# A hybrid gMLP and state-space block: the strips of squares of y are multiplied directly behind the products inside a chunk

## The chip, the cores and the metric

The kernel is one program on one core of a Trainium2 chip. The metric is the time of that core in microseconds, read on the device. Before the change it is 1373.79 us, the median of three runs between 1373.0 and 1373.83 us. TensorE is called PE in the profile (its weight loads have a row of their own, PEld), VectorE DVE, ScalarE ACT, GpSimd POOL, and SyncE, which issues most loads, SP.

## The reference

One layer on 1024 positions of width 1024. An input product feeds a chunked gMLP branch (`y_a`) and a Mamba-2 state-space branch (`y_b`); both are projected, gated, added and projected again.

```python
proj = h @ w_in
gm_u, gm_v, gm_z, ssm_z, xbc, dt_raw, g_a, g_b = jnp.split(proj, SPLITS, axis=-1)
y_a = spatial_gating(jax.nn.gelu(gm_u), jax.nn.gelu(gm_v), gm_ln_w, gm_ln_b, gm_ws, gm_bs) * jax.nn.silu(gm_z)
xbc = jax.nn.silu(causal_depthwise_conv(xbc, conv_w, conv_b))
...
y_b = ssd_scan(xh, dt, a, bm.reshape(b, s, SSM_GROUPS, SSM_STATE), cm.reshape(b, s, SSM_GROUPS, SSM_STATE))
y_b = y_b + xh * d_skip[:, None]
yz = (y_b.reshape(b, s, SSM_D_INNER) * jax.nn.silu(ssm_z)).reshape(b, s, SSM_GROUPS, SSM_D_INNER // SSM_GROUPS)
y_b = rms_norm(yz, ssm_norm_w.reshape(SSM_GROUPS, -1)).reshape(b, s, SSM_D_INNER)
merged = jax.nn.sigmoid(g_a) * (y_a @ w_proj_a) + jax.nn.sigmoid(g_b) * (y_b @ w_proj_b)
return x + gate[:, None, :] * (merged @ w_out)
```

and inside `ssd_scan`, with chunks of 128 positions, 8 groups (g), 4 heads to a group (r), head width 64 (p) and a state of 128 (n):

```python
cb = jnp.einsum('bclgn,bcsgn->bcgls', cc, bc)
y_diag = jnp.einsum('bcgls,bcgrls,bcsgrp->bclgrp', cb, decay, xd)
chunk_states = jnp.einsum('bcsgn,bcgrs,bcsgrp->bcgrpn', bc, decay_to_end, xd)
...
y_off = jnp.einsum('bclgn,bcgrpn,bcgrl->bclgrp', cc, prev_states, jnp.exp(a_cs))
return (y_diag + y_off).reshape(b, s, h, p)
```

The state passes from chunk to chunk as `state * chunk_decay + chunk_states`. The change touches how the mean of squares for the `rms_norm` of `yz` is got: one mean for every position and every group of 256 channels.

## The kernel before

**Stages.** The input products run first (to about 915 us), with the gMLP branch worked in beside them. The state-space stage follows, from about 915 to 1118 us; beside it PE works on the projection of `y_a` (tiles `pma`). Behind it come the projection of the normed `y_b` and the merge (`p1` to `p6` are its passes) and the last product.

**The state-space stage.** Eight groups run in pairs: `order` lists the steps, (group 2r, step s) and (group 2r + 1, step s) in turn, for r = 0 to 3 and s = 0 to 3. A step is 256 positions, two chunks. The loop over `order` does three things for a step and draws slices of the projection between them:

- `front(s)`: eight matmuls `yi`, the products inside a chunk (two chunks, four heads, output on 64 rows each), then `sp`, the increments of the states (two matmuls, one in the last step of a group). DVE adds `sp` to the state that POOL has decayed (`mul_state`, `add_state`), and forms `y` from `yi` and the skip term.
- `draw(4)` to `draw(6)`: so many slices of the projection, each two matmuls of 512 columns into `pma`.
- `back(s)`: four matmuls `yn`, the states carried in, and `evacuate`: DVE `ym`, then POOL two operations on `y` and `yz`.
- `prep` of the step after next: `pc` and `px`, transposes and the product of C and B.

A matmul of 32-bit floats leaves two records in the trace, and some are missing from it.

**The strips.** When two steps of a group are done (512 positions, half q), `post` stores `yz` to `yb_d`, and eight slots later ACT squares both 128-row halves in place (`squares`), three slots later POOL adds them (`sum`, L1252), and three slots later `post2` runs: four matmuls with a 128 x 32 block of ones, each over 128 positions, which sum the squares over the rows into strips of 32 rows of the tile `pq`. DVE evicts the tile (scale and EPS) into a row buffer, `cwt` for even and `tri` for odd groups (L1264), and a DMA from ACT's queue stores four rows of it to `ms_d`. After the second half SP loads `ssq` from `ms_d` (`post3`), POOL raises it to the power -1/2 (`root`, L1279), and ACT's queue stores it to `rs_d`. Groups 6 and 7 in their second half go another way (`late_squares`), at the end.

**What sets the order.** The order on PE, and on SP among its loads, is that of the program (`pin`). A slot is one call of `run_tasks`, at the end of `front`, `back` and `prep`; `later(d, f)` puts f in the list for the d-th slot from now. So `post2` runs at the end of an item, in all in-loop places at the end of a `front`, behind `sp`. DVE, ACT and POOL are ordered by the scheduler, with some operations tied by `link` and some raised by `tc.high_priority()`. `bank` hands out the PSUM tiles: `px` has two banks, all others take turns on six.

Where the trace of before shows `pq` of twelve places in the loop, they start at 965.80, 972.74, 990.66, 997.60, 1015.76, 1028.16, 1040.57, 1048.63, 1066.56, 1078.96, 1091.37 and 1098.30 us; four more stand at the end, from 1118.34 on. "Place" below means one of the twelve, in this order.

Of the kernel before, what the change touches and what calls it, by code (L numbers as in the profile page):

```python
# [8 lines left out]
F32 = mybir.dt.float32  # L9
# [7 lines left out]
P = 128  # L17
# [18 lines left out]
def hybrid_kernel(  # L36
# [481 lines left out]
    tasks = []  # L518
    slot = [0]

    def later(delay, f, *a):
        tasks.append((slot[0] + delay, f, a))
# [547 lines left out]

    NSET = 5
    nstep = [0]
    work, last = [], {}

    def link(key, f):
        if key in last:
# [16 lines left out]
    class Group:  # L1093
# [63 lines left out]
        def front(self, s):  # L1157

            g, nm = self.g, f"{self.g}_{s}"
            sl, dcy, bn, xd, xe, ea = self.pre[s]  # L1160
            yi = bank(f"yi{nm}")
            for i in range(2):
                for h in range(HPG):
                    j, hh = h // 2, h % 2
                    mm(yi[hh * HD : (hh + 1) * HD, j * 256 + i * P : j * 256 + (i + 1) * P],
                       xd[:, i * 256 + h * HD : i * 256 + (h + 1) * HD], dcy[:, h, i, :])
            sp = bank(f"sp{nm}")
            two = s < NCH // 2 - 1
            self.sts = [self.st]
            for i in range(2 if two else 1):  # L1170
                mm(sp[:, i * 256 : (i + 1) * 256], bn[:, i * P : (i + 1) * P], xe[:, i * 256 : (i + 1) * 256])
            self.add_state(s, 0, sp)
            if two:
                self.mul_state(s, 1)
            y1 = turn(y1_r, f"y1{nm}", F32).rearrange("p (j t) -> p j t", j=2)
            for j in range(2):
                link("V", lambda: V.scalar_tensor_tensor(y1[:, j], sl[:, 2 + j], dskt[:, 2 * g + j : 2 * g + j + 1],
                                           yi[:, j * 256 : (j + 1) * 256], op0=ALU.mult, op1=ALU.add))
            self.y[s] = y1
            if two:  # L1180
                self.add_state(s, 1, sp)
# [68 lines left out]

        def sum(self, q, sq):
            link("G", lambda: G.tensor_add(sq[0], sq[0], sq[1]))  # L1252
            later(3, self.post2, q, sq[:1])

        def post2(self, q, sq):

# [284 lines left out]
    for n in range(len(order)):  # L1541
# [7 lines left out]
        if n + 2 < len(order):  # L1549
            step(n + 2, "prep")  # L1550
        fetch(n + 6)
    while tasks or work:
        draw(2)
        run_tasks()
        beside_step()


    room.extend(ea_r[0] + [st_tag])
# [34 lines left out]
    first, rest = room[:3], room[10:21]  # L1593
# [188 lines left out]
    psb = ps3.__enter__()  # L1782
# [6 lines left out]
    for u, (nm, k) in enumerate(units):  # L1789
        if k == 0:  # L1790
            if nm == "p1":
                first = {t: psb.tile([P, 512], F32, name=f"{t}p", tag=f"b{t}") for t in ('y1', 'x0', 'x1', 'y3', 'y0', 'x2', 'x3', 'y2')}
                psx, psy = ([first[f"{v}{j}"] for j in range(4)] for v in "xy")
            elif nm in ("p5", "p2"):
                psy = banks(f"y{nm}", "y")
            ps = psy if nm in ("p2", "p5", "p3") else psx
        multiply(u, ps)
        ahead(u)
        if nm == "p1" and k == 2:
            for tags, _ in (y1_r, ym_r):  # L1800
                room.extend(tags)
        if nm == "p1" and k in (1, 4):
            for late in groups[NG - 2 :]:
                late.post4() if k == 4 else late.post3()
            if k == 1:
                for late in groups[NG - 2 :]:
                    late.root()
        if nm == "p2" and k == 4:
            room.extend(rb_r[0])
        if k % 2 and nm in GATES:  # L1810
            gate_load(GATES[nm][0] + k // 2, GATES[nm][1])
        if nm == "p4":
            for at, f, a in BESIDE:
                if at == k:
                    f(*a)
        if nm in ("p7", "p2", "p4") and k % 2 == (nm != "p4"):
            merged(*more.pop(0))
        if k == KT - 1:
            for j in range(4):
                with tc.high_priority():  # L1820
                    if nm in ("p1", "p3", "p5"):
                        t = slot_tile(f"{nm}_{j}")
                        A.copy(t, (psx if nm == "p1" else psy)[j])
                        sums[nm, j] = t
                    if nm == "p6":
                        V.tensor_add(sums["p3", j], sums["p3", j], psx[j])
                    elif nm == "p5":
                        V.tensor_add(sums["p3", j], sums["p3", j], sums["p5", j])
                        more.append((j, 1, sums["p3", j], f"p3_{j}"))
                    elif nm == "p7":  # L1830
                        V.tensor_add(sums["p5", j], sums["p5", j], psx[j])
                        more.append((4 + j, 1, sums["p5", j], f"p5_{j}"))
                    elif nm == "p2":
                        V.tensor_add(sums["p1", j], sums["p1", j], psy[j])
                        more.append((j, 0, sums["p1", j], f"p1_{j}"))
                    elif nm == "p4":
                        merged(4 + j, 0, None, None)
# [117 lines left out]
    for t in range(3):  # L1955
# [5 lines left out]
        if t == 0:  # L1961
            y0 = root(0)
# [7 lines left out]
    y2 = root(2)  # L1970
# [46 lines left out]
```

## Time and profile before

| | |
|---|---|
| median of three runs | 1373.79 us |
| the profiled execution | 1372.68 us |
| its span on the core | 1370.7 us |
| TensorE clock granted | 0.999 of full |
| state-space stage, 915 to 1118 us: PE, weight loads busy | 201.97, 168.30 us |
| the same: DVE, ACT, POOL busy | 165.00, 142.03, 165.29 us |
| matmuls of `pq` in the stage | 5.5 us busy, 285 ns each |
| POOL's sum of squares (L1252) | 14 of them, 1306 ns each |

The table's middle part is the view by windows: of each engine the busy time in a stretch of the span. The view of lines groups instructions by line, operation and tile, with the count, the busy time, the mean length of one, and the idle time ahead of them with what ended it. The timeline gives start and length of each instruction or of a run of equal ones; where such a run has a bracket, it stood idle for that long before, and the name behind the arrow ended it ("issue": nothing that the profile shows). The weight loads are shown apart from the matmuls, which they run beside.

### The profile page before, as it was taken

Reading aid. Unit: us, or ns where it says so; the run is one execution under the profiler, and the core shown is the slowest. Engines: PE = TensorE matmul, PEld = TensorE weight load, DVE = VectorE, ACT = ScalarE, POOL = GpSimd, SP = SyncE. Lnnn points to the kernel's source line nnn. Section 1 sums busy time; section 2 is a strip of 40 time slices with the busy share of each in tenths; the row PEclk is TensorE's granted clock in tenths of the full one; section 3 lists DMA queues with packets and bytes.
Section 4 is the critical chain, followed back from the end, with each engine's and each line's share of the span. In section 5 each row is a group of like instructions: output and inputs, shape, how many; then the busy total and the mean of one; then the engine's idle time right before and its main releaser. Section 6 shows DMA issues by size and latency. Waiting matters only on the chain.

```text
span 1370.7 us, 20173 instructions
## 1 busy us (share of the span) xinstructions
PE 1356.4 (99%) x6943; PEld 1114.6 (81%) x6943; DVE 1045.6 (76%) x1716; ACT 799.7 (58%) x1447; POOL 192.0 (14%) x191
## 2 busy tenths in 40 slices
PE   8999999999999999999999999999999999999997
PEld 7688888888888888888888888888888878788886
DVE  4786876777778889688897787468878856959976
ACT  5764656666657666466576665486867733333443
POOL 1000000000000000000000000016888871000002
PEclk9999999999999999999999999999999999999999
DMA  9675444333344657777666775489889858978913
GB/s 287 179 234 150 136 123 124 100 122 117 115 132 138 206 172 233 252 239 230 194 198 186 231 239 168 154 314 300 300 284 314 290 203 295 334 267 321 382 38 123
DMA packets 249530, 288.65 MB, mean 211 GB/s; under 512 B 16812, under 2 KB 196436, under 8 KB 249428
## 3 DMA queue, kind: packets, MB, share of 16 engines
q1 hardware_dynamic: 174868, 203.80, 46.3%
q10 hardware_dynamic: 74560, 83.57, 17.9%
q8 instruction: 55, 0.90, 0.3%
q14 instruction: 47, 0.39, 0.1%
HBM read 199.82 MB, written 87.49 MB: 210 GB/s over the span
## 4 chain that ended last, share of the span: by engine, by line
PE 87%; DVE 4%; DMA 3%; POOL 3%; ACT 1%; issue 1%; SPq 1%; POOLq 0%; ACTq 0%; DVEq 0%
PE xcb L565 6%; PE xz L565 6%; PE xx L565 6%; PE xuz L565 6%; PE xg L565 6%; PE pma L82 4%; PE ox L1861 3%; PE yuz L565 3%; PE ycb L565 3%; PE yp L1670 3%; PE yz L565 3%; PE vx L954 3%; PE yx L565 3%; PE yg L565 3%; PE yi L82 2%; PE sp L82 2%
## 5 line engine op out<-in xcount | busy, mean ns | idle before, releaser
L1123 POOL TENSOR_SCALAR_AFFINE_SELECT dcy<-dcy 128x1024 f32<-128x1024 f32 x32 | 35.4, 1106 | 791.5 <-DMA yl<-ya_d 747.2
L1131 ACT ACTIVATE dcy<-dcy,nacs 128x128 f32<-128x128 f32 x256 | 78.3, 389 | 3.6 <-POOL dcy L1123 3.2
L1147 DVE TENSOR_TENSOR dcy<-dcy,pc 128x1024 f32<-128x1024 f32 x32 | 39.0, 1219 | 9.2 <-PE pc L85 5.2
L1226 POOL TENSOR_TENSOR yz<-y,sl 128x512 f32<-128x512 f32 x32 | 43.8, 1369 | 2.5
L82 PE MATMUL pma<-yh,wah 128*128 128x512 f32 x128 | 42.7, 415 | 0.0
L82 PE MATMUL pma<-yh,wal 128*128 128x512 f32 x128 | 42.3, 412 | 0.0
L1154 ACT COPY bn<-pc 128x256 f32<-128x256 f32 x32 | 11.9, 371 | 50.7 <-DVE dcy L1147 48.3
L82 PE MATMUL pma<-yl,wah 128*128 128x512 f32 x128 | 40.1, 394 | 0.0
L1608 DVE SCALAR_TENSOR_TENSOR yn<-yn,par,rb 128x512 f32<-128x512 f32 x32 | 24.3, 760 | 20.6 <-DMA yn<-yb_d 18.8
L1119 ACT ACTIVATE ea<-dcy 64x512 f32<-64x512 f32 x64 | 39.8, 622 | 0.4
L1024 ACT ACTIVATE ac<-ac 128x1024 f32<-128x1024 f32 x32 | 33.9, 1060 | 9.4 <-DVE ac L1022 9.2
L1225 POOL TENSOR_TENSOR y<-y,ym 128x512 f32<-128x512 f32 (+1 forms) x32 | 37.4, 1169 | 2.1 <-DVE ym L1223 2.1
L1223 DVE TENSOR_TENSOR ym<-yn,ea 128x512 f32<-128x512 f32 (+1 forms) x32 | 19.9, 621 | 21.7 <-PE yn L82 21.7
L1022 DVE SCALAR_TENSOR_TENSOR ac<-c2x,cwt,ac 128x1023 f32<-128x1023 f32 (+2 forms) x24 | 30.7, 1279 | 6.3 <-ACT ac L1020 6.2
L82 PE MATMUL yi<-dcy,xd 128*64 128x128 f32 x512 | 35.0, 279 | 0.0
L1022 DVE SCALAR_TENSOR_TENSOR ac<-c2cb,cwt,ac 128x1023 f32<-128x1023 f32 (+2 forms) x24 | 30.6, 1275 | 5.6 <-ACT ac L1020 5.5
L1876 POOL TENSOR_TENSOR r<-r,fnw 128x512 f32<-128x512 f32 x4 | 5.3, 1345 | 206.3 <-ACT junk L1874 206.3
L986 ACT ACTIVATE vm<-vm,vr 128x128 f32<-128x128 f32 x64 | 25.8, 483 | 13.6 <-DMA vm<-v_d 13.1
L824 ACT CAST wbb<-wbr 128x512 fp32r<-128x512 f32 x32 | 19.8, 619 | 22.2 <-DMA wb_d<-wbb 16.2
L82 PE MATMUL sp<-xe,bn 128*128 128x256 f32 x112 | 32.7, 409 | 0.0
L82 PEld LDWEIGHTS yn<-sl,st 128*128 128x128 f32 x224 | 29.8, 191 | 2.8 <-POOL st L1189 0.4
L82 PEld LDWEIGHTS yi<-dcy,xd 128*64 128x64 f32 x512 | 27.3, 136 | 5.7 <-issue 2.9
(2963 smaller groups left out, 4372.6 us busy)
## 6 DMA issues: line engine op xcount, KB each, us to landing
sl<-s_d SPq DMA_DIRECT2D x32, 768.0 KB
s_d<-ac ACTq DMA_DIRECT2D x32, 512.0 KB
wb_d<-wbb ACTq DMA_DIRECT2D x32, 512.0 KB
dcy<-acs_d SPq DMA_DIRECT2D x32, 512.0 KB
av<-in_w_in_dram SPq DMA_DIRECT2D x36, 256.0 KB
aw<-in_ada_w_dram SPq DMA_DIRECT2D x16, 512.0 KB
wbr<-in_w_proj_b_dram SPq DMA_DIRECT2D x32, 256.0 KB
yb_d<-yz ACTq DMA_DIRECT2D x32, 256.0 KB
```

Of the source, the lines that this page charges most:

```text
L82: pin(PE.matmul(acc, l, r, start=first, stop=last))
L565: pin(PE.matmul(ps, lw[:, k * P : (k + 1) * P], r[k], start=first and n + k == 0, stop=n == 2 and k == 3, skip_group_check=not first))
L954: pin(PE.matmul(ps[pn][j], l[:, j * P : (j + 1) * P], r, start=nm in ("p1", "p5", "p2") and n + units[i][1] == 0, stop=n == 2 and k == 3, ...
L1022: V.scalar_tensor_tensor(ac[:, s:], cc[:, : S - s], conv_wt[:, 3 - s, i : i + 1], ac[:, s:], op0=ALU.mult, op1=ALU.add)
L1119: link("A", lambda: A.activation(ea[hh * HD : (hh + 1) * HD], dcy.rearrange("p (j e) i l -> p e j (i l)", e=2)[hh * HD : (hh + 1) * HD, hh ...
L1123: link("G", lambda: G.affine_select(out=d8, in_=d8, compare_op=ALU.is_ge, fill=-1e30, base=0, pattern=[[0, 2 * HPG], [1, P]], channel_mult ...
L1131: link("A", lambda: A.activation(dcy[:, h, i, :], dcy[:, h, i, :], AF.Exp, bias=sub[:, i, h : h + 1]))
L1147: link("V", lambda: V.tensor_tensor(d3, d3, pc[:, 0:256].unsqueeze(1).to_broadcast([P, HPG, 256]), op=ALU.mult))
L1225: link("G", lambda: G.tensor_add(y1[:, :, t0:], y1[:, :, t0:], m[:, :, t0:]))
L1226: link("G", lambda: G.tensor_mul(yz, y1, sl[:, 4:6]))
L1670: pin(PE.matmul(ps[j], a[:, v, js], r, start=first and n + k == 0, stop=n == 2 and k == KT - 1, skip_group_check=not first))
L1861: pin(PE.matmul(ps, a[:, tsl], b[:, cs], start=first and n + j == 0, stop=n == 2 and j == 3, skip_group_check=not first))
```

## The change

`sum` no longer puts `post2` itself into the list, but, one slot sooner, a call that appends it to the list `posts`. `front` empties that list between `yi` and `sp`; the loop at the end of the stage empties it too. So in twelve places the four strip matmuls stand between `yi` and `sp` instead of behind `sp`. The tiles `pq` and `sp` are handed out in the other order, and what hangs on `post2` by a delay, the load of `ssq`, comes one slot earlier. The list of names in `first` gives the first eight PSUM tiles of the next stage their banks in another order.

```diff
--- before.py
+++ after.py
@@ -1070,7 +1070,7 @@
 
     NSET = 5
     nstep = [0]
-    work, last = [], {}
+    work, last, posts = [], {}, []
 
     def link(key, f):
         if key in last:
@@ -1164,6 +1164,9 @@
                     j, hh = h // 2, h % 2
                     mm(yi[hh * HD : (hh + 1) * HD, j * 256 + i * P : j * 256 + (i + 1) * P],
                        xd[:, i * 256 + h * HD : i * 256 + (h + 1) * HD], dcy[:, h, i, :])
+            while posts:
+                p, q, sq = posts.pop(0)
+                p.post2(q, sq)
             sp = bank(f"sp{nm}")
             two = s < NCH // 2 - 1
             self.sts = [self.st]
@@ -1250,7 +1253,7 @@
 
         def sum(self, q, sq):
             link("G", lambda: G.tensor_add(sq[0], sq[0], sq[1]))
-            later(3, self.post2, q, sq[:1])
+            later(2, posts.append, (self, q, sq[:1]))
 
         def post2(self, q, sq):
 
@@ -1549,10 +1552,13 @@
         if n + 2 < len(order):
             step(n + 2, "prep")
         fetch(n + 6)
-    while tasks or work:
+    while tasks or work or posts:
         draw(2)
         run_tasks()
         beside_step()
+        while posts:
+            p, q, sq = posts.pop(0)
+            p.post2(q, sq)
 
 
     room.extend(ea_r[0] + [st_tag])
@@ -1789,7 +1795,7 @@
     for u, (nm, k) in enumerate(units):
         if k == 0:
             if nm == "p1":
-                first = {t: psb.tile([P, 512], F32, name=f"{t}p", tag=f"b{t}") for t in ('y1', 'x0', 'x1', 'y3', 'y0', 'x2', 'x3', 'y2')}
+                first = {t: psb.tile([P, 512], F32, name=f"{t}p", tag=f"b{t}") for t in ('x0', 'x1', 'x2', 'y3', 'y0', 'y1', 'y2', 'x3')}
                 psx, psy = ([first[f"{v}{j}"] for j in range(4)] for v in "xy")
             elif nm in ("p5", "p2"):
                 psy = banks(f"y{nm}", "y")
```

PE, the second place (group 1, steps 0 and 1; `pq_0`, `sp_0`, `yi_0` are the tiles of the step, `pma` the projection's):

```order
 L85 MATMUL px_0_8972<-ident,sl_0_8745 128x128 x2
 L82 MATMUL yi_0_8994<-dcy_0_8669,xd_0_8898 64x128 x8
-L82 MATMUL sp_0_9003<-xe_0_8900,bn_0_8902 128x256 x2
-L82 MATMUL pq_0_9012<-yz_0_8479,ones 32x128 x4
+L82 MATMUL pq_0_9003<-yz_0_8479,ones 32x128 x4
+L82 MATMUL sp_0_9010<-xe_0_8900,bn_0_8902 128x256 x2
 L82 MATMUL pma_0_8796<-yh_8106,wal_0_8547 128x512
 L82 MATMUL pma_1_8799<-yh_8107,wal_0_8547 128x512
```

The strips went from behind `sp` to ahead of it; nothing else moved. The other eleven places read alike.

PE near the eighth place, the matmuls from the last slice of the projection to `prep` of group 5, step 2 (`pc5_2`), with what they wait for by the program. Before:

```order
L82 MATMUL pma4_0_9683<-yl50_8133,wah4_1_9364 128x512
L82 MATMUL pma4_1_9686<-yl51_8134,wah4_1_9364 128x512
L82 MATMUL yn5_1_9938<-sl5_1_9556,st22_8262 128x128 x2
L82 MATMUL yn5_1_9938<-sl5_1_9556,st_8259 128x128 [waits DVE_49]
L82 MATMUL yn5_1_9938<-sl5_1_9556,st_8259 128x128
L82 MATMUL pc5_2_9950<-sl5_2_9722 128x128 [waits DMAHW5_49,DVE_49]
L85 MATMUL pc5_2_9950<-ident_135,sl5_2_9722 128x128
```

Now:

```order
L82 MATMUL pma4_0_9683<-yl50_8133,wah4_1_9364 128x512
L82 MATMUL pma4_1_9686<-yl51_8134,wah4_1_9364 128x512
L82 MATMUL yn5_1_9938<-sl5_1_9556,st22_8262 128x128 x2
L82 MATMUL yn5_1_9938<-sl5_1_9556,st_8259 128x128 [waits DVE_49]
L82 MATMUL yn5_1_9938<-sl5_1_9556,st_8259 128x128
L82 MATMUL pc5_2_9950<-sl5_2_9722 128x128 [waits DMAHW6_49,PE_49]
L85 MATMUL pc5_2_9950<-ident_135,sl5_2_9722 128x128
```

The order here is the same. The bank that `pc5_2` takes was left by `sp5_1` before, and the wait on DVE is for the state sum that reads `sp5_1`; now it was left by `pq2_1`, whose eviction is covered by the wait on DVE two rows up.

SP, the loads around `ssq` of groups 0 and 1 (`ms_d_66` and `ms_d_67`; `dcy` and `sl` are the loads of a later step):

```order
 L91 DMA tha_0_9270<-th_d 128x512
 L91 DMA tha_1_9273<-th_d 128x512
-L91 DMA dcy_0_9314<-acs_d 128x1024
-L91 DMA sl_0_9316<-s_d_125 128x1536
 L91 DMA ssq<-ms_d_66 128x8
-L91 DMA dcy_0_9402<-acs_d 128x1024
-L91 DMA sl_0_9404<-s_d_126 128x1536
+L91 DMA dcy_0_9315<-acs_d 128x1024
+L91 DMA sl_0_9317<-s_d_125 128x1536
 L91 DMA ssq<-ms_d_67 128x8
+L91 DMA dcy_0_9403<-acs_d 128x1024
+L91 DMA sl_0_9405<-s_d_126 128x1536
```

Each load of `ssq` stands one pair of `dcy` and `sl` earlier; the same happens for groups 2 and 3. On DVE the eviction of a strip stands ahead of the step's state sum in the twelve places, and in the next stage four of the six low halves `p6bl` stand one operation later. On ACT the store to `ms_d` stands ahead of two stores to `yb_d` in six places. POOL's order is the same. The last two strips in the old late order, those of groups 6 and 7 in their first half, stand together at the end, four to five slices of the projection later.

## The prediction

> **What bounds the kernel now.** First the page: its head and its busy row.
>
> ```profile
> span 1370.7 us, 20173 instructions
> PE 1356.4 (99%) x6943; PEld 1114.6 (81%) x6943; DVE 1045.6 (76%) x1716; ACT 799.7 (58%) x1447; POOL 192.0 (14%) x191
> ```
>
> TensorE is busy all but 14 us of the span and sets its end. POOL's 14% is an average that misleads here: the view by windows shows the state-space stage (about 915 to 1118 us) apart. Its columns are busy time and count of PE, PEld, DVE, ACT and POOL, then clock and DMA.
>
> ```profile
> 1015.00:1025.00 10.00, 9.84 (x72) 8.03 (x73) 7.80 (x16) 7.79 (x23) 9.84 (x9) 1.00 0.80 272
> ```
>
> In this stretch POOL is as full as PE. Third, what PE waited for from 905 to 1180 us:
>
> ```profile
> PE pc L82 <- DVE st L1197: 0.9, 1, 0.9
> PE pq L82 <- POOL yz L1244: 0.7, 1, 0.7
> PE pq L82 <- POOL yz L1252: 0.2, 1, 0.2
> ```
>
> Three waits, under 2 us together. So a microsecond of PE's own work in the stage is a microsecond of the kernel, as long as the others keep up. The 0.7 is the last strip of all, which stays where it is.
>
> PE's own work has a hidden part, though. The timeline of PE, a step with strips and the next one without, then the weight loads of the same two steps:
>
> ```profile
> 970.65 1.09 PE L82 MATMUL yi<-dcy,xd 128*64 128x128 f32 x16
> 971.67 1.13 PE L82 MATMUL sp<-xe,bn 128*128 128x256 f32 x4
> 972.74 0.43 PE L82 MATMUL pq<-yz,ones 128*32 128x128 f32 x8
> 973.09 0.74 PE L82 MATMUL pma<-yh,wal 128*128 128x512 f32 x2
> 973.67 0.63 PE L82 MATMUL pma<-yh,wah 128*128 128x512 f32 x2
> ...
> 976.72 1.09 PE L82 MATMUL yi<-dcy,xd 128*64 128x128 f32 x16
> 977.74 1.13 PE L82 MATMUL sp<-xe,bn 128*128 128x256 f32 x4
> 978.52 0.81 PE L82 MATMUL pma<-yh,wah 128*128 128x512 f32 x2
> 979.17 0.63 PE L82 MATMUL pma<-yl,wah 128*128 128x512 f32 x2
> ```
>
> ```profile
> 970.65 0.85 PEld L82 LDWEIGHTS yi<-dcy,xd 128*64 128x64 f32 x16 [0.17 <-issue]
> 971.67 0.73 PEld L82 LDWEIGHTS sp<-xe,bn 128*128 128x128 f32 x4 [0.17 <-issue]
> 972.73 0.16 PEld L82 LDWEIGHTS pq<-yz,ones 128*32 128x32 f32 x8 [0.33 <-issue]
> 973.09 0.30 PEld L82 LDWEIGHTS pma<-yh,wal 128*128 128x128 f32 x2 [0.20 <-issue]
> ...
> 978.50 0.41 PEld L82 LDWEIGHTS pma<-yh,wah 128*128 128x128 f32 x2
> ```
>
> In these rows 128\*64, 128\*32 and 128\*128 are the part of the array that a matmul uses. Wherever that shape changes, the next weight load stands idle for 0.17 to 0.33 us and waits for nothing else; where it stays (sp to pma, both 128\*128) there is no idle time. A step with strips has four changes, one without has two.
>
> **The change, part by part.**
>
> *The strips' place on PE.* From yi's first matmul to the second pair of pma, by which both steps run evenly again, is 973.67 - 970.65 = 3.02 us with strips and 979.17 - 976.72 = 2.45 without: strips cost 0.57 where they stand. Moved, the order is yi, pq, sp, pma, with three changes of shape. Pieced from the rows: 1.02 from yi to the next shape (971.67 - 970.65), 0.35 from strips to a 128\*128 group (973.09 - 972.74), 1.43 from sp to the second pair (979.17 - 977.74). That is 2.80, so 0.22 less in each place.
>
> This takes it that 128\*64 to 128\*32 is a change like the others. No row shows that pair. Upper end: no pause there, and the strips stream behind yi. Their row above covers 0.43 us, of which the last matmul's own duration is 0.285:
>
> ```profile
> L82 PE MATMUL pq<-yz,ones x128: 272/285/297, 965.8 to 1131.0; 128*32 128x128 f32 x128
> L1264 DVE TENSOR_SCALAR tri<-pq x8: 276/280/283, 974.2 to 1133.7; 128x128 f32<-128x128 f32 x8
> ```
>
> So they add 0.14 instead of 0.35, and a place gains 0.43. Lower end: the pause behind strips is the longest seen, 0.33 instead of 0.17, which leaves 0.06. I take 0.22: every change of shape in the rows pauses, whichever way it goes.
>
> The Trainium skill (TensorEngine Tiling (Array Packing), Key Properties) says that a change of tiling mode, not merely of tile, drains the engine, and lists 128x64 and 128x32 as separate modes. By that rule a place gains 0.22, without it 0.43. The trace agrees for the four pairs it has, with 0.17 to 0.33 us, and has no row for this one.
>
> *Nine of the twelve moved places.* A strip also needs POOL's sum of squares, and now it is wanted some 1.07 us earlier, at the old start of sp. Nearest rows, POOL's sums against PE, places in the order of the text below:
>
> ```profile
> 968.54 1.27 POOL L1252 TENSOR_TENSOR yz<-yz 128x512 f32<-128x512 f32 x1
> 1014.43 1.27 POOL L1252 TENSOR_TENSOR yz<-yz 128x512 f32<-128x512 f32 x1
> 1038.23 1.29 POOL L1252 TENSOR_TENSOR yz<-yz 128x512 f32<-128x512 f32 x1
> 1045.28 1.27 POOL L1252 TENSOR_TENSOR yz<-yz 128x512 f32<-128x512 f32 x1
> 1064.05 1.27 POOL L1252 TENSOR_TENSOR yz<-yz 128x512 f32<-128x512 f32 x1
> ```
>
> ```profile
> 1014.90 0.70 PE L82 MATMUL sp<-xe,bn 128*128 128x256 f32 x2
> 1015.76 0.42 PE L82 MATMUL pq<-yz,ones 128*32 128x128 f32 x8 [0.16 <-POOL yz L1252]
> 1039.51 1.13 PE L82 MATMUL sp<-xe,bn 128*128 128x256 f32 x4
> 1045.25 0.49 PE L82 MATMUL pc<-sl 128*128 128x128 f32 x2 [0.87 <-DVE st L1197]
> 1049.56 0.62 PE L82 MATMUL pma<-yh,wah 128*128 128x512 f32 x2
> 1065.93 0.70 PE L82 MATMUL sp<-xe,bn 128*128 128x256 f32 x2
> ```
>
> The sum is done 1.86 us ahead at the second place (971.67 - 969.81) and 0.61 at the ninth (1065.93 - 1065.32). That is more than the 0.22 by which PE gains on POOL between two of them, and POOL's next work hangs on PE through yn, so it moves along. Seven other places have between 0.6 and 1.6. The fifth place is late by 0.80 (1015.70 against 1014.90), the seventh level (1039.52 against 1039.51). I count nine places free: the first five, by the next paragraph, and the last four. 9 x 0.22 = 1.98 us.
>
> *The loads of ms_d.* Since the strips come one slot sooner, the load of ssq for groups 0 to 3 stands ahead of a dcy and an sl load on SP.
>
> ```profile
> 999.54 0.32 SPq L91 DMA_DIRECT2D dcy<-acs_d  x1
> 1001.26 0.38 SPq L91 DMA_DIRECT2D ssq<-ms_d  x1
> ```
>
> ```profile
> 1008.14 1.66 POOL L1279 TENSOR_TENSOR ssq<-ssq,nhalf 128x8 f32<-128x8 f32 x1 [2.17 <-DMA ssq<-ms_d]
> ```
>
> POOL stood 2.17 us for that load, and the fifth place's sum is queued behind. Issued ahead of 999.54, the load is at least 1.72 us sooner, and the 0.80 by which this sum is late is covered. PE's present stall there goes too: sp to strips is 0.86 there (1015.76 - 1014.90), where sp's own 0.70 less the 0.06 by which such rows overlap (971.67 + 1.13 against 972.74) would be 0.64, so 0.2. If POOL gains nothing, the place loses 0.8 instead. Behind the earlier ssq wait dcy and sl, which are fetched five steps, some 30 us, before their step; a hold of 2 us is hidden by that.
>
> *The middle three places and the bank.* pc of group 5, step 2, waited 0.87 us for the state sum that frees its PSUM bank (its row in the pair of lists in the section on the change: of its two waits the one for DVE becomes one for PE); now that bank is left by a strip, emptied earlier. This stall goes. But POOL's sum for the eighth place ends at 1046.55 whatever PE does, since the chain behind it runs through DVE, ACT and POOL from about 1020. Strips at 1046.60, 0.35 to sp, 1.43 to the second pair: 1048.38, against 1049.56. The stretch gains 1.2 us in place of 0.87 + 3 x 0.22. Ends: 0.7 if that chain slides by half a microsecond, 1.7 if it keeps ahead.
>
> *What lies beside.* The eviction of a strip, 0.28 us on DVE, goes ahead of the state sum in all twelve places; DVE is 78% busy in the window above, the second state sum waits for POOL anyway, so nothing; 12 x 0.28 = 3.4 us if DVE were the bound. On ACT the store of ms_d goes ahead of two stores of yb_d that wait for POOL: nothing. The two last strips that now stand together save two changes, but the end waits for the yb_d store (the 0.7 above): nothing. In the next stage DVE's order shifts around the lows that PE waits for. PE's wait and the DVE rows ahead of it:
>
> ```profile
> 1194.65 0.19 PEld L1670 LDWEIGHTS x0p<-p6bl,p6a 128*128 128x128 f32 x1 [0.77 <-DVE p6bl L1646]
> ```
>
> ```profile
> 1193.91 1.29 DVE L1646 TENSOR_TENSOR p6bl<-yn,p6bh 128x512 fp32r<-128x512 f32 x2
> ```
>
> Two operations take 1.29 there, so one is about 0.6. One goes ahead of four of the six lows of this pass, the one PE waited 0.77 for keeps its place in DVE's order. If PE comes to it up to 0.6 later because of an earlier low, most of that is taken out of the 0.77, and what is left I put at +0.2 us, between nothing and 0.6.
>
> **Sum.** -1.98 - 0.2 - 1.2 + 0.2 = -3.2 us. The profiled execution took 1372.68 us, 1.98 of it around the span; the sum makes it 1369.5. The median of the runs shown, 1373.79, lies 1.1 above that execution, so the forecast for the median is 1370.6. Its own range: 0.06 a place with 0.7 in the middle gives -1.2; 1.7 in the middle gives -3.7: 1370.1 to 1372.6.
>
> **Rivals.**
>
> *No pause between the two narrow shapes.* 9 x 0.43 = 3.9 instead of 1.98, the rest the same, since the middle is held by POOL: -5.1, 1368.7 us. For it: both shapes use columns of the array only. Against it: four pairs of shapes, four pauses.
>
> *The gain is eaten, no change.* The pause is long (0.06 a place) or POOL's and DVE's chain from 1020 gives back what PE wins: -1.2 or less, 1372.6. For it: POOL at 9.84 of 10 in the window. Against it: PE waits at one place only in 200 us for more than 0.3.
>
> *The strips hold the states, slower.* Until now a late sum held only strips and the projection. Now sp is queued behind the strips, DVE's state sum behind sp, POOL's state product behind that, and the next sum behind all. With POOL's sums L later against PE than in the rows, the waits are the sum of L minus each place's margin: for L = 1.2 some 2.0 at the fifth, 1.2 at the seventh, 0.6 at each of the first, sixth and ninth, 0.6 at the rest, 5.6 in all; against it stand 12 x 0.22 and 1.0 for the stalls, so about +1.9: 1375.7. It decides from L = 0.9 on. Against it: POOL's work is neither more nor in another order, and loses a wait of 2.17.
>
> **How the numbers follow.** Forecast 0.54, no pause 0.20, eaten 0.12, slower 0.14. A measurement of this kernel tells 0.2%, 2.75 us, from no change. Two thirds of the forecast's range and the no-pause case pass that: 0.36 + 0.20 = 0.56 faster; 0.18 + 0.12 = 0.30 within; 0.14 slower. The range for 8 in 10 runs from the no-pause case with the 1.7 of the middle (-5.6, 1368.2), less 0.4 for half the spread of the three runs, to the eaten case with nothing left: 1367.8 to 1373.8.
>
> **What would show it.** Right: PE's weight load of pq idles about 0.17 behind yi, that of sp about as long behind pq, none before pma; yi to the second pma pair is 2.80; no wait before pc near 1045; no POOL wait for ssq near 1008. Rival one: no idle before pq and 2.59. Wrong: pq waiting for POOL yz at more than three places, or yn or pc for DVE st.

## The result, and the profile after

The changed kernel takes 1369.13 us, the median of six runs (1367.37 to 1370.38), against 1373.81 us of the kernel before in six runs (1373.0 to 1377.12) on the same chip. The ratio is 0.9962, with a 95% interval of 0.995 to 0.9975: 4.7 us, or 0.34%, faster. The forecast was 1370.6 us with a range of 1367.8 to 1373.8. The profiled execution took 1367.94 us, 4.74 less than that of before, and is the one read here.

The head of the page of the changed kernel, and then all that PE waited for between 905 and 1240 us, where the kernel before had the three waits shown in the prediction and a fourth in the next stage:

```profile
span 1366.0 us, 20176 instructions
PE 1352.3 (99%) x6943; PEld 1116.6 (82%) x6943; DVE 1045.9 (77%) x1716; ACT 799.2 (59%) x1447; POOL 192.5 (14%) x191
```

```profile
PE pq L82 <- POOL yz L1247: 1.4, 2, 0.8
```

PE is 4.1 us shorter busy (1352.3 against 1356.4) with the same count of 6943 matmul records. That row also covers pauses of the weight load, so what is work and what is waiting is read from the rows below. The wait of pc for DVE is gone. What is left are two waits for the late sums of groups 6 and 7, where there was one.

To see where the time went, the start times of four kinds of matmul are set beside each other: the first yi of the state-space stage, the last yi, the first x0p of the next stage, and the first matmul of its fifth pass, p7. From there to the end both kernels take the same (142.07 us to the start of the last matmul).

| from, to | before | after | difference |
|---|---|---|---|
| start to first yi | 914.66 | 915.43 | +0.77 |
| loop: first yi to last yi | 198.82 | 194.88 | -3.94 |
| end of the stage: last yi to first x0p | 19.25 | 19.71 | +0.46 |
| next stage: first x0p to p7 | 89.03 | 87.04 | -1.99 |

The first row is no part of the change: nothing moved there, and over the profiles of this study the first yi starts anywhere between 914.5 and 918.8 us. That is why the runs below are compared by medians of 5 to 11 runs, and their stages by times counted from the first yi.

The loop can be read step by step. Between the starts of two yi lies one step; the twelve steps that hold strips (the "places"), in us, in one profile each:

| place | 1 | 2 | 3 | 4 | 5 | 6 | 7 | 8 | 9 | 10 | 11 | 12 |
|---|---|---|---|---|---|---|---|---|---|---|---|---|
| before | 6.50 | 6.07 | 6.93 | 6.50 | 6.72 | 6.48 | 8.06 | 6.47 | 6.50 | 6.48 | 6.93 | 6.50 |
| after | 6.30 | 5.81 | 6.73 | 6.26 | 6.29 | 6.27 | 6.72 | 6.26 | 6.29 | 6.28 | 6.72 | 6.26 |

Ten places give 0.20 to 0.26 us each, the fifth 0.43, the seventh 1.34; that is 3.95 in all. The other steps of the loop agree within 0.02 us. Place 2 in the timeline of the changed kernel, matmuls and then weight loads:

```profile
971.21 1.09 PE L82 MATMUL yi<-dcy,xd 128*64 128x128 f32 x16
972.23 0.43 PE L82 MATMUL pq<-yz,ones 128*32 128x128 f32 x8
972.59 1.13 PE L82 MATMUL sp<-xe,bn 128*128 128x256 f32 x4
973.37 0.81 PE L82 MATMUL pma<-yh,wal 128*128 128x512 f32 x2
974.02 0.62 PE L82 MATMUL pma<-yh,wah 128*128 128x512 f32 x2
...
972.23 0.16 PEld L82 LDWEIGHTS pq<-yz,ones 128*32 128x32 f32 x8 [0.17 <-issue]
972.59 0.73 PEld L82 LDWEIGHTS sp<-xe,bn 128*128 128x128 f32 x4 [0.20 <-issue]
973.34 0.41 PEld L82 LDWEIGHTS pma<-yh,wal 128*128 128x128 f32 x2
```

From yi to the second pair of pma it is 974.02 - 971.21 = 2.81 us (forecast 2.80, before 3.02). The weight load idles 0.17 us ahead of pq and 0.20 ahead of sp, and not at all ahead of pma: three changes of shape, as said.

The middle and the load of ssq, again from the timeline of the changed kernel (POOL and PE):

```profile
1005.78 1.66 POOL L1282 TENSOR_TENSOR ssq<-ssq,nhalf 128x8 f32<-128x8 f32 x1
1012.89 1.28 POOL L1255 TENSOR_TENSOR yz<-yz 128x512 f32<-128x512 f32 x1
1043.25 0.39 PE L82 MATMUL pc<-sl 128*128 128x128 f32 x2
1043.77 1.27 POOL L1255 TENSOR_TENSOR yz<-yz 128x512 f32<-128x512 f32 x1
1045.46 0.43 PE L82 MATMUL pq<-yz,ones 128*32 128x128 f32 x8
```

POOL no longer stands for ssq (no bracket at 1005.78), pc no longer for its bank, and the sum of the eighth place ends at 1045.04, 0.42 ahead of its strips. The forecast had held it at 1046.55.

The end of the stage gives something back, and the next stage brings something that the forecast did not have. First the two late strips in the changed kernel:

```profile
1124.37 0.43 PE L82 MATMUL pq<-yz,ones 128*32 128x128 f32 x8 [0.57 <-POOL yz L1247]
1128.17 0.42 PE L82 MATMUL pq<-yz,ones 128*32 128x128 f32 x8 [0.84 <-POOL yz L1247]
```

Then the view of waits of the weight loads, before, for the lows of the passes p6 and p3; in the changed kernel neither row exists:

```profile
PEld x0p L1670 <- DVE p6bl L1646: 1.5, 3, 0.8
PEld y0p L1670 <- DVE p3bl L1646: 1.0, 3, 0.5
```

What feeds those lows are loads on SP, and one of them, rb12, reads what the store `rs_d6` (the factors of group 6) has written. POOL's root of group 6, that store and rb12, before:

```profile
1141.93 2.63 POOL L1279 TENSOR_TENSOR ssq<-ssq,nhalf 128x8 f32<-128x8 f32 x1 [11.11 <-DMA ssq<-ms_d]
1147.27 0.33 ACTq L94 DMA_DIRECT2D rs_d<-ssq  x1
1153.53 0.32 SPq L91 DMA_DIRECT2D rb<-rs_d  x1
```

And in the changed kernel:

```profile
1138.03 2.12 POOL L1282 TENSOR_TENSOR ssq<-ssq,nhalf 128x8 f32<-128x8 f32 x1 [9.92 <-DMA ssq<-ms_d]
1140.51 0.34 ACTq L94 DMA_DIRECT2D rs_d<-ssq  x1
1147.51 0.32 SPq L91 DMA_DIRECT2D rb<-rs_d  x1
```

Before, the store left 2.7 us behind the end of its root (1147.27 against 1144.56); now it leaves 0.4 behind it. ACT was not what held it, as it had nothing else to do in between. The chip's program names the reason. In it DMAs take their completion semaphores (the counters that tell of a landing) in turn, eight of them, and one that takes a semaphore waits until the DMA eight places ahead of it has landed. The store's own row, before and now:

```
L94 DMA rs_d6_64<-ssq_158 128x8 [waits DMAHW3_49,Pool_49]
L94 DMA rs_d6_64<-ssq_158 128x8 [waits DMAHW2_49,Pool_49]
```

Before, the DMA eight places ahead was the load rb8, which SP issues at 1143.28 us; now it is the load of ssq of group 7, since the store came to stand one DMA earlier in the program, ahead of a load for p3 instead of behind it. No line of the diff touches that store or that load; why the scheduler turned the two round was not followed.

The semaphore events of the traces bear this out. Before, the last part of rb8 lands at 1147.20 us and the store leaves at 1147.27; the store lands at 1153.51, and rb12 leaves at 1153.53. Now the load of ssq lands at 1140.43 and the store leaves at 1140.51; it has landed at 1144.35, 3.2 us before rb12 leaves. The runs below with a held store (e1, e3, e10) show the same: the store leaves 0.07 us behind the landing of rb8, and rb12 0.02 to 0.06 behind the landing of the store. The store of group 7 (`rs_d7`) is held in the changed kernel too, 2.3 us behind its root; what that costs no run shows.

### The profile page after: what moved, and what is told of

It reads as the page before. It is cut to its first block, busy times and chain, and to the rows that moved or that the text cites. A ratio compares the mean times of both kernels' runs of the same rounds, so it can differ in the third digit from the quotient of the medians.

```text
span 1366.0 us, 20176 instructions
## 1 busy us (share of the span) xinstructions
PE 1352.3 (99%) x6943; PEld 1116.6 (82%) x6943; DVE 1045.9 (77%) x1716; ACT 799.2 (59%) x1447; POOL 192.5 (14%) x191
## 4 chain that ended last, share of the span: by engine, by line
PE 92%; DMA 3%; DVE 2%; ACT 1%; SPq 1%; issue 0%; POOL 0%; POOLq 0%; DVEq 0%; ACTq 0%
PE xz L565 6%; PE xcb L565 6%; PE xx L565 6%; PE pma L82 6%; PE xuz L565 6%; PE xg L565 6%; PE ox L1867 3%; PE ycb L565 3%; PE vx L954 3%; PE yp L1676 3%; PE yz L565 3%; PE yx L565 3%; PE yg L565 3%; PE yuz L565 3%; PE yi L82 2%; PE sp L82 2%
```

## The experiments

The theory behind the runs: every change of array shape costs PE about 0.2 us and the move saves one in each place; the bank order removes the stall of pc; the next stage gains because the store of `rs_d6` is no longer held. The main rival for the last point: the next stage gains only because the stage ahead of it ends earlier.

**e1: strips behind sp again, the rest of the change kept.**

```diff
-            while posts:
-                p, q, sq = posts.pop(0)
-                p.post2(q, sq)
             sp = bank(f"sp{nm}")
...
                 mm(sp[:, i * 256 : (i + 1) * 256], bn[:, i * P : (i + 1) * P], xe[:, i * 256 : (i + 1) * 256])
+            while posts:
+                p, q, sq = posts.pop(0)
+                p.post2(q, sq)
```

> The changed kernel with the strips multiplied behind sp again and pq handed its bank behind sp; the earlier load of ssq and the new list of first banks stay. Theory (places 0.21 us each by one shape change fewer; the bank order removes the 0.87 us stall; the next stage gains 2.0 us because the store rs_d6 waits for an earlier DMA): all three are undone, so 1373 to 1374, yi to the second pma pair 3.02 us, the stall of pc near 1045 back, the store rs_d6 held 2 to 3 us behind its root. Rival (the gain of the next stage comes from the earlier ssq loads or the list of banks): 1371 to 1372, no wait for p6bl in the next stage.

Measured: 1373.39 us, ratio to before 0.9997 (0.9988 to 1.0006). The places are those of before within 0.1 us, with one exception: the fifth takes 6.50 in place of 6.72, which is what the earlier load of ssq is worth by itself. The stall of pc is back:

```profile
PE pc L82 <- DVE st L1200: 0.8, 1, 0.8
```

The root of group 6 ends at 1143.53 and its store leaves at 1146.86. So the place of the strips, with the order of banks that goes with it, carries the gain, directly or by what follows from it; the earlier load and the new list of banks bring next to nothing without it.

**e2: as e1, but pq takes its PSUM bank ahead of sp.**

```diff
+            mine = posts[:]
+            del posts[:]
+            for p, q, sq in mine:
+                p.pq = rows_bank[0](f"pq{p.g}_{q}")
             sp = bank(f"sp{nm}")
...
+            for p, q, sq in mine:
+                p.post2(q, sq)
```

> As e1, but pq is handed its PSUM bank ahead of sp, as in the changed kernel, while its matmuls stay behind sp. In this program the store rs_d6 waits for the load of ssq of group 7, as in the changed kernel, not for the load rb8 as before. Theory: places still cost 3.02 us, no stall of pc near 1045 (-1.1 us), next stage -1.5 to -2.0 us: about 1370.7, 2.6 to 3.1 below e1. Rival (the next stage is faster only because the state-space stage ends earlier, the bank order alone brings 0.9): 1372.5 to 1373, waits for p6bl in the next stage stay.

Measured: 1371.78 us, ratio 0.9986 (0.9977 to 0.9995), 1.6 below e1. The seventh place takes 7.16 where e1 takes 7.96, with no wait of pc: the bank order alone is worth 0.8 us. The other places are those of e1, but for the ninth and tenth, which are 0.1 and 0.2 longer. The next stage takes 88.04 us (e1: 88.64), and the store leaves 0.02 us behind its root. The theory had expected another microsecond here, and the time lies between what it and its rival gave; the profiled execution, at 1374.43 us the slowest of the eleven, also waited 1.2 us for a state ahead of the first strips.

**e3 and e4: the changed kernel with one small load more, ahead of the store (so that it waits for rb8 again), or behind it.**

```diff
+        def post3_again(self):
+            load(self.columns(), ms_d[self.g].rearrange("o (p c) -> (o p) c", p=P))
...
             load(f32(t), wb_d[k][:, WB[nm]])
+            if (nm, k) == ("p3", 0):
+                groups[0].post3_again()
```

In e4 the condition is ("p3", 3).

> The changed kernel with one more small load on SP (ssq of group 0 again, 128x8), between the loads for p3, step 0 and step 1, so that the store rs_d6 waits for the load rb8, eight DMAs earlier, instead of ssq of group 7. Theory: rs_d6 leaves 2 to 3 us behind its root, rb12 with it, and PE waits for the lows of p3 and p6 again, 1.5 to 2.0 us: 1370.7 to 1371.2. Rival (the wait of that store is covered, the gain comes from the earlier end of the state-space stage): 1369.1 to 1369.5, no waits for the lows.

> Control for e3: the same small load, but behind the store rs_d6 (with the loads for p3, step 3), so that rs_d6 waits for ssq of group 7 as in the changed kernel. Theory and rival both: the time of the changed kernel, 1369.1 to 1369.5; if it comes out like e3, the extra load itself is the cost and not the wait.

Measured: e3 1369.59 us, ratio 0.9965 (0.9951 to 0.9979); e4 1368.51 us, 0.9960 (0.9947 to 0.9972). The medians differ by 1.1 us, the intervals overlap, and the time of e3 lies 1.1 us below the theory's range and close to the rival's. By the times alone nothing is decided; the traces tell more. Root and store of group 6 in e3:

```profile
1138.73 2.07 POOL L1285 TENSOR_TENSOR ssq<-ssq,nhalf 128x8 f32<-128x8 f32 x1 [10.63 <-DMA ssq<-ms_d]
1144.00 0.33 ACTq L94 DMA_DIRECT2D rs_d<-ssq  x1
```

Held 3.2 us, and the waits for the lows are back, here in the view of waits:

```profile
PE y0p L1681 <- DVE p3bl L1657: 0.6, 1, 0.6
PE x0p L1681 <- DVE p6bl L1657: 0.6, 1, 0.6
```

In e4 the store leaves at once (1140.75), and only a wait of 0.5 us for p6bl is left. The next stage begins as early in e3 as in the changed kernel (1130.00 against 1130.02), and yet takes 88.96 us, against 87.96 in e4. So in these two profiles the held store goes with about 1 us of the next stage, less than the 1.5 to 2.0 that were expected.

**e5: strips of 64 rows, the shape of yi.** The last two matmuls overwrite the first two, so half of the means of squares are those of other positions.

```diff
-                mm(pq[32 * i : 32 * i + 32, 0:P], ones[:, 0:32], sq[0][:, i * P : (i + 1) * P])
+                mm(pq[64 * (i % 2) : 64 * (i % 2) + 64, 0:P], ones[:, 0:64], sq[0][:, i * P : (i + 1) * P])
```

> The changed kernel with strips of 64 rows, the array shape of yi: the four matmuls use 64 columns of ones and the last two overwrite the first two, so the means of squares of half the positions are those of other positions. Theory (the pause comes from the change of shape): no idle time of the weight load between yi and pq, one of 0.17 to 0.20 us between pq and sp; eight records more at yi's rate (0.85 us for 16) make yi to the second pma pair 0.85 x 1.5 + 0.17 + 1.43 = 2.88, 0.07 more than in the changed kernel, about +1 us in all: 1370. Rival (the pause comes with any new group of operands): idle 0.17 before pq too, 3.05 us a place, +3 us: 1372.

Measured: 1371.41 us, ratio 0.9983 (0.9974 to 0.9992). The weight loads of place 2:

```profile
972.57 0.85 PEld L82 LDWEIGHTS yi<-dcy,xd 128*64 128x64 f32 x16 [0.17 <-PE pc L85]
973.38 0.47 PEld L82 LDWEIGHTS pq<-yz,ones 128*64 128x64 f32 x8
974.03 0.73 PEld L82 LDWEIGHTS sp<-xe,bn 128*128 128x128 f32 x4 [0.17 <-issue]
```

No idle time between yi and pq, 0.17 us ahead of sp, and 2.89 us from yi to the second pair of pma (expected 2.88). The operands are as new as before, only the shape is the same: the pause belongs to the change of shape. Each place is 0.10 us longer than in the changed kernel, since wider strips take longer than a pause saves. Beside that one step waited 0.6 us for POOL, and the late strips 1.4 us; with these the time is nearer to the rival's than the mechanism is.

**e6: the changed kernel with the load of ssq one slot later, where it was.**

```diff
-                later(3, self.post3)
+                later(4, self.post3)
```

> The changed kernel with the load of ssq of groups 0 to 3 one slot later, where it was before the change. Theory (POOL waits for that load near 1005 us, and the sum of the fifth place is queued behind): the strips of the fifth place wait for POOL 0.5 to 1.0 us, a POOL wait of about 2 us for ssq is back; 1369.8 to 1370.1. Rival (POOL's lead covers it, the earlier load brings nothing): no wait of pq for POOL in the loop, 1369.1.

Measured: 1370.74 us, ratio 0.9977 (0.9968 to 0.9986). POOL's wait and the strips of the fifth place:

```profile
1010.48 1.66 POOL L1282 TENSOR_TENSOR ssq<-ssq,nhalf 128x8 f32<-128x8 f32 x1 [2.51 <-DMA ssq<-ms_d]
1016.77 1.28 POOL L1255 TENSOR_TENSOR yz<-yz 128x512 f32<-128x512 f32 x1
1018.10 0.42 PE L82 MATMUL pq<-yz,ones 128*32 128x128 f32 x8 [1.12 <-POOL yz L1255]
```

The fifth place takes 7.47 us in place of 6.29, and all other places are unchanged. The median is 0.6 us above the theory's range; in the profile the next stage, too, is 0.5 longer (87.59). So the move needs the earlier load: without it, 1.2 of the 3.9 us would be lost again.

**e7: the strips of the first halves of two groups together.**

```diff
-            while posts:
+            while posts and (len(posts) > 1 or posts[0][1]):
                 p, q, sq = posts.pop(0)
                 p.post2(q, sq)
+                if posts and not q:
+                    p, q, sq = posts.pop(0)
+                    p.post2(q, sq)
```

> The changed kernel with the strips of the first halves of a pair of groups (0 and 1, 2 and 3, 4 and 5) multiplied together, the first of them held one step. Theory (a place costs 0.36 us, of which 0.13 is the extra change of shape; the second of two strips that stand together costs 0.22): -0.14 us for each of three pairs, -0.4: 1368.7. Rival (the strip held back frees its buffer later or shifts the banks, so that a wait comes in): same or slower, 1369.1 to 1370.5, with a wait of yn, pc or POOL in the places named.

Measured: 1371.25 us, ratio 0.9986 (0.9977 to 0.9995). The pair of groups 4 and 5 does what was expected: 5.94 and 6.48 us in places 9 and 10, against 6.29 and 6.28, 0.15 less. The first two pairs run into new waits, by the view of waits:

```profile
PE sp L82 <- ACT bn L1154: 1.3, 1, 1.3
PE pq L82 <- DVE xe L1150: 1.2, 1, 1.2
```

and lose about 1.2 us each, so that the time is above even the rival's range. Why bn and xe are late there was not followed further.

**e8: the late strips one and two slices of the projection later.**

```diff
-    draw(left[0] - 8)
+    draw(left[0] - 7)
...
-            draw(left[0] - 3)
+            draw(left[0] - 1)
```

> The changed kernel with the strips of the late squares one and two slices of the projection later (left 7 and 1 in place of 8 and 3). Theory (PE comes 3.2 us earlier to the end of the stage, the late sums only 1.0 to 2.4, so PE waits 0.57 and 0.84 us there): the waits shrink to 0.1 and 0.3 to 0.6 us, -0.6 to -1.0: 1368.1 to 1368.5. Rival (the store of the means of groups 6 and 7 is late then, and the next stage's loads with it): the waits move to the lows of p3 and p6, 1369.1 or more.

Measured: 1369.82 us, ratio 0.9973 (0.9962 to 0.9984). The end of the stage takes 18.59 us, 1.1 less than in the changed kernel, and the next stage 89.48, 2.4 more. This is the rival's case. PE came to p1 earlier and stood there, 1.2 us, and then for a low of p6, by the waits of the weight loads:

```profile
PEld x0p L1676 <- DVE p6bl L1652: 1.2, 2, 1.0
PEld x0p L1676 <- DVE p1a L1657: 0.8, 2, 0.4
PEld x0p L1676 <- DVE p1bl L1652: 0.7, 2, 0.4
```

So what this run saves at the end of the stage is waited out behind it.

**e9 and e10: the kernel before, with one load left out ahead of the store, or behind it.** In e9 group 5 uses the factors of group 4 in the second half of the positions, in e10 group 7 those of group 6.

```diff
-        if n % 2 == 0:
+        if n == 10 and h:
+            rbs[5, 1] = rbs[4, 1]
+        elif n % 2 == 0:
```

In e10 the numbers are 14, 7 and 6.

> The kernel before the change without the load rb10 (the factors of group 4 are used for group 5 in the second half of the positions). With one DMA fewer between, the store rs_d6 waits for ssq of group 7 as in the changed kernel, not for rb8; the state-space stage is the old one. Theory (the held store costs about 1 us of the next stage): rs_d6 leaves at once behind its root, the next stage from the first matmul of p1 to that of p7 takes 87.0 to 88.0 us in place of 89.0; 1372.4 to 1372.9. Rival (the next stage gains only when the stage ahead of it ends earlier): 88.6 to 89.0 us, 1373.4 to 1373.8, like e10.

> Control for e9: the kernel before the change without the load rb14 (the factors of group 6 are used for group 7 in the second half of the positions), which stands behind the store rs_d6, so that this store still waits for rb8. Theory and rival both: rs_d6 held 2 to 3 us, 88.6 to 89.0 us from p1 to p7, 1373.4 to 1373.8; if it comes out like e9, the load left out is the gain and not the wait.

Measured: e9 1373.16 us, ratio 0.9993 (0.9984 to 1.0001); e10 1373.78 us, 0.9999 (0.999 to 1.0008). Roots and stores of e9:

```profile
1142.86 1.83 POOL L1279 TENSOR_TENSOR ssq<-ssq,nhalf 128x8 f32<-128x8 f32 x1 [11.05 <-DMA ssq<-ms_d]
1145.19 4.04 ACTq L94 DMA_DIRECT2D rs_d<-ssq  x2
```

and of e10:

```profile
1142.77 2.44 POOL L1279 TENSOR_TENSOR ssq<-ssq,nhalf 128x8 f32<-128x8 f32 x1 [10.32 <-DMA ssq<-ms_d]
1148.82 2.26 ACTq L94 DMA_DIRECT2D rs_d<-ssq  x2
```

In e10 the store is held 3.6 us behind the root's end (1145.21), in e9 0.5. The state-space stage is the old one in both. The next stage takes 87.27 us in e9 and 88.08 in e10, 0.8 apart, without any help from an earlier end of the stage ahead. In e9 no wait for the lows of p3 and p6 is left, in e10 one of 0.6 us. Together with e3, where the stage ahead ends early and the next one is long all the same, this speaks against the rival as the only cause. The evidence is limited: these are single profiles, e9 also takes a load out of SP's queue ahead of rb12 while e10 takes one out behind it, and e10's next stage came out below the 88.6 to 89.0 expected. The medians are 0.6 apart, which the intervals do not separate, and e9's lies between what theory and rival gave.

**e11: the changed kernel with the old list of first PSUM banks of the next stage.**

```diff
-    for t in ('x0', 'x1', 'x2', 'y3', 'y0', 'y1', 'y2', 'x3')
+    for t in ('y1', 'x0', 'x1', 'y3', 'y0', 'x2', 'x3', 'y2')
```

> The changed kernel with the old list of first PSUM banks of the next stage. Theory (the list brings nothing by itself, or saves a wait of PE for the eviction of the last strip): x0, x1 or x2 waits up to 0.4 us for DVE at the start of p1, 1369.1 to 1369.5. Rival (the list carries a part of the next stage's gain): waits for the lows of p3 and p6 are back, 1370 or more.

Measured: 1376.77 us, ratio 1.0019 (1.001 to 1.0029): slower than before, and 6.7 us above the changed kernel on the same chip (e12). Neither the theory nor its rival had this. The matmuls around the start of p1, and the operation of DVE that one of them waits for:

```profile
1131.62 0.39 PE L1676 MATMUL x1p<-p1bh,p1a 128*128 128x512 f32 x1
1138.17 0.80 PE L1676 MATMUL x2p<-p1bh,p1a 128*128 128x512 f32 x1 [6.17 <-DVE tha L1488]
1138.76 0.63 PE L1676 MATMUL x2p<-p1bl,p1a 128*128 128x512 f32 x1
1141.75 0.58 PE L1676 MATMUL x0p<-p1bh,p1a 128*128 128x512 f32 x1
1142.17 0.39 PE L1676 MATMUL x1p<-p1bh,p1a 128*128 128x512 f32 x1
...
1136.84 1.28 DVE L1488 SCALAR_TENSOR_TENSOR tha<-tha,pma 128x512 f32<-128x512 f32 x2
```

With the strips in their new order the ring of banks stands elsewhere at the end of the stage. By the old list x2 falls on a bank of the last product of the projection (`pma`), which DVE reads only at 1136.84, behind the lows of p1. In the changed kernel DVE reads the last product about as late (1136.16), but the new list gives that bank to a tile that is not needed until p3. So the line in the diff that looks like a detail is a condition of the gain.

**e12: the changed kernel once more.**

> The changed kernel once more, on the same chip as e9 to e11, to see how far the next stage varies by itself. Theory: 1368.6 to 1369.6, state-space loop 194.9 us from the first yi to the last; p1 to p7 between 87.0 and 88.0 us. Rival (the profile of the changed kernel was a favourable execution): 88.5 us or more there, with waits for the lows, 1369.6 to 1370.5.

Measured: 1370.08 us (1367.08 to 1370.24, five runs), ratio 0.9964 (0.9951 to 0.9976). Loop 195.06 us, every place within 0.01 of the first profile, end of the stage 19.32, next stage 87.06. The first profile was no exception.

All profiles together, by whether the store of `rs_d6` is held, for the next stage from x0p to p7. Left out are e11, where PE stands 6.2 us in p1, and e8, whose store is not held and whose stage takes 89.48 us, 1.2 of the excess in p1 and 1.3 behind it:

| store | next stage, us | mean |
|---|---|---|
| held 2.7 to 3.6 us | before 89.03, e1 88.64, e3 88.96, e10 88.08 | 88.68 |
| not held | after 87.04, e12 87.06, e7 87.14, e5 87.15, e9 87.27, e6 87.59, e4 87.96, e2 88.04 | 87.41 |

The two groups just do not overlap (88.08 against 88.04), and with e8 they would. The difference of the means is 1.3 us: 0.9 among the kernels with strips behind sp (before, e1, e10 against e2, e9), 1.6 among those with strips ahead of it (e3 against the rest). A held store is not the only thing that makes PE wait here: e4, not held, has the same wait of the weight load for p6bl as e10, held, 1.0 us.

## Why the prediction came out as it did

The direction and the range were right, and the mechanism in the loop. The sum was -3.2 us and the profile shows -5.5 behind the first yi. That the time still fell inside the range owes something to luck: the range reached so far down for the sake of a rival that did not come true, and the gain of the next stage was not in it; the misses in the middle and at the end of the stage, 0.56 and 0.46 us, happen to cancel. By its steps:

- **The strips' place, 0.22 us each: right.** Measured 0.20 to 0.26, by the three changes of shape. The pause between yi and strips that no row showed is there, 0.17 us, and e5 shows that it goes when the shape is the same. With it the rival without a pause falls; its time (1368.7) came nearer to the result than the forecast's, but for another reason. The rule of the Trainium skill (TensorEngine Tiling (Array Packing), Key Properties) that a change of tiling mode drains the engine agrees with e5: 0.17 us of idle weight load at the change of mode, none where the mode stays.
- **The loads of ms_d, 0.2 us: right.** The fifth place gains 0.43, 0.22 more than a plain one; e1 gives the same 0.22 with the strips left behind sp. The loss without the earlier load was put at 0.8 and is 1.2 (e6).
- **The middle, 1.2 us: the mechanism was right, the limit was wrong.** The three places gave 0.21 + 1.34 + 0.21 = 1.76. The bank order took the stall of pc away, 0.8 us by itself (e2). The step that failed is that the sum of the eighth place would end at 1046.55 "whatever PE does": it ended at 1045.04, in an execution that had begun the stage 0.77 later. POOL's chain moved along with PE here as it does at the other places.
- **The end of the stage, nothing: off by 0.46 us.** PE came 3.2 us earlier and the late sums only 1.0 and 2.4, so two waits, 0.57 and 0.84, stand where one of 0.73 stood. In e12, the same kernel, they are 0.76 and 0.28, and this end takes 19.32 us against 19.25 before; so most of the 0.46 lies within what one kernel varies by. e8 shows that these waits cannot simply be filled.
- **The next stage, +0.2 us: wrong in sign, and the largest error.** It looked at DVE's order alone, and so failed to see what the lows wait for. PE's waits for the lows of p3 and p6 are gone, and the stage is 1.99 us shorter in the profile. That the store of `rs_d6` stood behind another DMA's semaphore, and rb12 behind the store, is shown by the landings; what it costs is an estimate from single profiles, 0.8 (e9 against e10) to 1.3 us (the means of the table). The remaining 0.7 to 1.2 us is not settled: it is about as much as the next stage varies among kernels whose store is not held (87.04 to 88.04).
- **The list of banks: not in the sum.** The prediction did not price it. It brings nothing by itself, but left out it would have turned the change into a loss of 0.19%, 2.6 us (e11).
- **The slower rival, strips holding up the states:** no strip in the loop waits for POOL in the changed kernel. e6 shows how near it is: one late load, and place 5 loses 1.2 us. The rival had assumed that such a loss spreads to later places; in e6 it did not.

Loop, end and next stage together make -3.94 + 0.46 - 1.99 = -5.47, the later start of the stage takes 0.77 of it back in this pair of executions, and -4.7 is what the spans of this pair show. That the medians show -4.7 too is partly chance: they mix executions with early and late starts, and on the chip of e12 they lie 4.1 apart (1370.08 against 1374.20).

## What to carry to other kernels

Where small matmuls of another array shape must stand between large ones, count the changes of shape and put the small ones where a change is due anyway: here it was about a fifth of a microsecond each time (0.17 to 0.33), and the profile shows it as idle time of the weight load that waits for nothing. When the order of tiles from a ring of banks changes, follow the ring to its end, since the next user of each bank is another one. And a DMA that leaves late although its data are ready may be standing behind the semaphore of an unrelated DMA; in this program it was the one eight places ahead.

## What the runs showed of the hardware that was not expected

When PE had stood for 6.2 us in e11, its clock went down and stayed down after it resumed. The view by windows of e11, with PE's busy time and count, granted clock, DMA share and GB/s:

```profile
1132.00:1134.00 2.00, 0.01 (x1) 1.00 0.60 99
1136.00:1138.00 2.00, 0.00 (x0) 0.50 0.92 319
1140.00:1141.00 1.00, 1.00 (x4) 0.50 0.07 4
1142.00:1143.00 1.00, 1.00 (x5) 0.93 1.03 156
```

By the clock's own record it was at half from 1135.32 to 1142.15 us: it fell 3.3 us behind the end of the last matmul (1132.01) and rose 4.0 us behind the start of the next (1138.17). In those 4.0 us a matmul of 512 columns came about every 0.43 us, and every 0.23 from then on. So the wait of 6.2 us cost 8.3 between the first matmuls of p1 and of p3 (30.08 us against 21.76). The Trainium skill (TensorE: Matmul & The Clock Gate, What's actually happening) has the clock at half rate after an idle window of about 3.4 us and back after about as long a busy one; the trace agrees with it, with 3.3 and 4.0 us. The waits of PE in the other profiles, up to 1.4 us in this stretch, left the clock at 1.00.
